# Sixteen state readouts in a decoder step: four fused multiply-sums on VectorE become one wide product there and four summing copies on ScalarE

## The chip, the cores and the metric

The kernel runs on one core of one Trainium2 chip. The metric is the device time of one execution in microseconds (us), as the median of several runs; smaller is better. The core has a matrix engine (TensorE, PE in the profile), a vector engine (VectorE, DVE), a scalar engine (ScalarE, ACT), GpSimd (POOL) and SyncE (SP), which issues most of the DMA transfers here. Each engine works through its own stream of instructions in order, and the engines meet at semaphores.

## The reference, cut to what matters

One step of a decoder trunk: a half-step SwiGLU FFN, a mixer (causal pooling beside a Mamba-2 SSD scan), a second half-step FFN, a final RMSNorm. It is computed for 512 prompt tokens and for 8 sample sequences of one new token each. Their 520 columns go through all products together. The sample rows have a stored SSD state of their own, 16 heads x 64 x 128 per sequence, and for one token the scan is one update and one readout:

```
h_new = exp(dt*A) * h0 + (dt * x) outer B          # per sequence b, head, 64 x 128
y     = sum over the 128 states n of  C[n] * h_new[.., n]
      = exp(dt*A) * (sum_n C[n] * h0[.., n]) + (dt * x) * (sum_n B[n] * C[n])
```

The kernel uses the second form of `y`. The sum over n of `C[n] * h0[.., n]` is the **readout** that is changed. B and C are shared by the heads of a group, of which there are two.

## The kernel before, in words

Features lie on the partitions, tokens along the free dimension, in two halves of 260 columns. Products with large weights are split: a weight tile is loaded raw by SP (`load_unit`, L111 to L114), `split` writes its rounded high part on ScalarE (L107) and the remainder on VectorE (L108), and three matmuls (`mm3`, L117 to L119) replace an fp32 product. Three high and three low buffers hold a unit each, so the cast of a unit can run once the unit three before it has been used.

The mixer's order is written out by hand as plans. The change works within this one:

```python
GATE_PLAN = (
    "A4 z0 B3 z1 m3 z2 B4 z3 s2 A5 z4 s2 B5 A6 z5 s2 s2 G0 z6 A7 z7 B6 s2 o0 H0 s2 o1 B7 s2 o2 s2 G1 "
    "o3 g0 g1 H1 g2 g3"
)
```

- `z` is a product of the gate's input projection, evacuated by two multiplications on VectorE (L916). `A` and `B` are the two halves of an SSD chunk: `ssd_a` makes decay matrices by exponentials on ScalarE (L861 to L871) and a large product on VectorE (L877), `ssd_b` multiplies with them on PE and combines on VectorE (L899 to L907).
- `s2` does two samples. `sample(b, g)` (L789) loads the row C of sequence b and group g, repeated over all partitions (`cb`, 128x128, L791), and the four 128x128 state blocks of that group (`h0`, L793), and reads out each block into one column of `ysm`: one VectorE instruction per block that multiplies, writes the product to a tile nobody reads (`junk`) and gives the row sums (L796). In the profile each is two rows, SCALAR_TENSOR_TENSOR and DVE_READ_ACCUMULATOR. There are 16 samples (8 sequences by 2 groups), so 64 readouts. `h0` has four buffers, `cb` shares three with other small tiles.
- `G` (`gate`, L932) begins with `sample_y`, which combines the readouts of one group (L802 to L804), adds them to the sample columns of X (L940) and multiplies by the gate (L942). `G0` needs the first eight samples, `G1` the last eight.
- `H` (`gate_out`, L944) takes squares on ScalarE (L948), sums them over partitions with a matmul of ones (`psr_y`, L161), makes the reciprocal root (L162 on ScalarE, L163 on VectorE) and writes the normalized, split operand `catg` (L955 to L957).
- `o`, `g`, `h` are output products over the pooling part, the first and the second half of the SSD part: units of four groups of 12 matmuls, each group added into the residual on VectorE (L926). `g` needs the `catg` of H0. `h`, which opens the last plan (`LAST_PLAN`), needs that of H1.

A planner lays out every engine's stream when the kernel is built: it plays the program against its own costs for instructions and takes, on each engine, the earliest instruction of the program that is ready by its clock. So an engine's stream isn't the program's order, and it is fixed before the run. `tc.keep_in_program_order(ins)` pins an instruction behind the one that the program issued last on the same engine. Later instructions may still be planned between pinned ones. Each of the 64 readouts is pinned so, behind the readout or other VectorE instruction before it.

Of the kernel before, what the change touches and what calls it, by code (L numbers as in the profile page):

```python
# [11 lines left out]
AF = mybir.ActivationFunctionType  # L12
ALU = mybir.AluOpType
# [3 lines left out]
P = 128  # L17
# [543 lines left out]
def mixer(tc, ins, outs, e):  # L561
    nc = tc.nc
# [191 lines left out]
    ysm = mp.tile([P, NX, NS], F32, tag="ysm", name="ysm")  # L754
    sbc = mp.tile([P, 2, NS], F32, tag="sbc", name="sbc")
    junk = act.tile([P, NT], F32, tag="acc", name="junk")[:, :P]
    scr_bc = dr.tile([NS, 512], F32, name="scr_bc")

    def rows_bc(b, a, g):
        return scr_bc.rearrange("b (a g n) -> b a g n", a=2, g=2)[b, a, g].unsqueeze(0).to_broadcast([P, P])  # L760
# [28 lines left out]
    def sample(b, g):  # L789
        cb = tmp.tile([P, HB], F32, tag="ta", name=f"cb{b}{g}")[:, :P]  # L790
        nc.sync.dma_start(out=cb, in_=rows_bc(b, 1, g))  # L791
        h0 = mp.tile([P, 4, P], F32, tag="h0", bufs=4, name=f"h0_{b}{g}")
        nc.sync.dma_start(out=h0, in_=ins["state_ssm"][:, b, 4 * g : 4 * g + 4])  # L793
        for q in range(4):
            tc.keep_in_program_order(
                nc.vector.scalar_tensor_tensor(out=junk, in0=h0[:, q], scalar=1.0, in1=cb, op0=ALU.mult, op1=ALU.mult,  # L796
                                               accum_out=ysm[:, 4 * g + q, b : b + 1]))

    def sample_y(g):
        gs = slice(4 * g, 4 * g + 4)  # L800
# [161 lines left out]
    def samples(n):  # L962
        for _ in range(n):
            if smp:
                sample(*smp.pop(0))
# [134 lines left out]
```

## Time and profile before

| | |
|---|---|
| median of 3 runs | 1006.09 us (1003.35, 1006.09, 1006.34) |
| the profiled execution | 1003.51 us, of which the span is 1000.5 us |
| mean granted TensorE clock | 0.994 |
| busy: PE, VectorE, ScalarE, GpSimd | 971.7, 806.9, 528.7, 87.8 us |
| instructions on VectorE and ScalarE | 1408 and 881 |

The span runs from the first to the last instruction of the profiled execution; 3 us of its time lie outside. Busy time is an average over stages with different limits, so the stretch in which the changed lines run has to be looked at for itself. Matmuls overlap one another, and a busy PE row says only that some matmul was under way. In timelines the columns are the start in us, the duration in us, the engine and line, the operation, the tiles and shapes, the number of merged instructions, and in brackets the idle time before the row and what ended it. In tables by stretch, each row has the length of the stretch and then the busy us of each engine in it, with the number of instructions.

### The profile page before, as it was taken

What the parts mean: (1) busy time and instruction counts of PE and PEld (TensorE: products, weight loads), DVE (VectorE), ACT (ScalarE), POOL (GpSimd) and SP (SyncE); (2) the same over time, 40 slices, a digit from 0 to 9 for tenths busy, and PEclk for the clock granted to TensorE, in tenths of its full rate; (3) what the DMA queues carried; (4) which work ended last, traced back from release to release, by engine and by line L of the source; (5) the groups of instructions that cost most, each with busy time, mean ns of one, the idle gap of its engine ahead of it and who ended that gap; (6) DMA issues with size and microseconds to landing.
All of it is one profiled execution on the core that took longest, in us unless ns stands there. A gap on an engine that the chain in (4) does not pass through costs nothing.

```text
span 1000.5 us, 19362 instructions
## 1 busy us (share of the span) xinstructions
PE 971.7 (97%) x7850; PEld 951.4 (95%) x7850; DVE 806.9 (81%) x1408; ACT 528.7 (53%) x881; POOL 87.8 (9%) x157
## 2 busy tenths in 40 slices
PE   7999999999999999999999999999999999999994
PEld 6899999999999999999899998899999999999993
DVE  7999657996569688788979987999957999668865
ACT  7566414664145455684845235666743666436552
POOL 0000000000000000167312000100012000120000
PEclk9999999999999999999999999999999999999997
DMA  6333232323223223263334421423346333452213
GB/s 194 112 126 114 98 101 73 124 88 124 85 85 106 85 104 117 87 216 105 107 133 122 146 90 54 124 94 118 127 137 187 120 127 118 124 195 96 95 33 85
DMA packets 44072, 114.44 MB, mean 114 GB/s; under 512 B 6408, under 2 KB 15560, under 8 KB 43984
## 3 DMA queue, kind: packets, MB, share of 16 engines
q1 hardware_dynamic: 40912, 103.78, 30.7%
q0 software_dynamic: 3072, 9.44, 3.5%
q8 instruction: 61, 1.00, 0.4%
q14 instruction: 27, 0.22, 0.1%
HBM read 105.86 MB, written 7.34 MB: 113 GB/s over the span
## 4 chain that ended last, share of the span: by engine, by line
PE 88%; DVE 6%; ACT 2%; POOL 2%; issue 1%; DMA 0%; SPq 0%; DVEq 0%; ACTq 0%
PE A L119 8%; PE A L117 8%; PE A L118 8%; PE dn L117 7%; PE dn L119 7%; PE dn L118 7%; PE BE L117 6%; PE BE L119 6%; PE BE L118 6%; PE P L232 4%; PE wo L117 2%; PE wo L118 2%; PE wo L119 2%; PE inz L117 2%; PE inz L119 2%; PE inz L118 2%
## 5 line engine op out<-in xcount | busy, mean ns | idle before, releaser
L117 PE MATMUL dn<-g,whi_1d 128*128 128x260 f32 x352 | 99.3, 283 | 0.2 <-DVE td L367 0.2
L118 PE MATMUL dn<-g,whi_1d 128*128 128x260 f32 x352 | 99.5, 283 | 0.0
L119 PE MATMUL dn<-g,wlo_1d 128*128 128x260 f32 x352 | 99.4, 283 | 0.0
L367 DVE SCALAR_TENSOR_TENSOR td<-dn,r_f 128x520 f32<-128x520 f32 x40 | 27.9, 699 | 73.2 <-PE dn L119 73.2
L119 PE MATMUL dn<-g,wlo_2d 128*128 128x260 f32 x256 | 72.4, 283 | 0.0
L118 PE MATMUL dn<-g,whi_2d 128*128 128x260 f32 x256 | 72.3, 282 | 0.0
L117 PE MATMUL dn<-g,whi_2d 128*128 128x260 f32 x256 | 72.3, 282 | 0.0
L117 PEld LDWEIGHTS dn<-g,whi_1d 128*128 128x128 f32 x352 | 66.1, 188 | 0.4 <-DVE td L367 0.4
L118 PEld LDWEIGHTS dn<-g,whi_1d 128*128 128x128 f32 x352 | 66.3, 188 | 0.0
L119 PEld LDWEIGHTS dn<-g,wlo_1d 128*128 128x128 f32 x352 | 66.2, 188 | 0.0
L297 ACT COPY ac<-A 128x260 f32<-128x260 f32 x123 | 45.6, 374 | 29.3 <-PE A L119 28.0
L107 ACT CAST whi_1d<-raw_1d 128x1024 fp32r<-128x1024 f32 (+1 forms) x24 | 23.4, 980 | 67.0 <-PE dn L118 54.2
L260 DVE TENSOR_TENSOR s<-raw 128x1024 f32<-128x1024 f32 x41 | 50.0, 1220 | 3.9 <-DMA raw<-in_w2gu 3.9
L232 PE MATMUL P<-xg_f,raw 128*128 128x260 f32 x192 | 45.1, 392 | 6.2 <-DMA raw<-in_w1gu 5.4
L232 PEld LDWEIGHTS P<-xg_f,raw 128*128 128x128 f32 x192 | 36.9, 195 | 12.1 <-ACT xg_f L179 5.4
L117 PEld LDWEIGHTS dn<-g,whi_2d 128*128 128x128 f32 x256 | 48.3, 189 | 0.0
L118 PEld LDWEIGHTS dn<-g,whi_2d 128*128 128x128 f32 x256 | 48.2, 188 | 0.0
L119 PEld LDWEIGHTS dn<-g,wlo_2d 128*128 128x128 f32 x256 | 48.2, 188 | 0.0
L118 PE MATMUL wo<-catg,whi_wo 128*128 128x260 f32 x128 | 36.4, 285 | 1.3 <-DVE catg L957 1.3
L117 PE MATMUL wo<-catg,whi_wo 128*128 128x260 f32 x128 | 37.3, 292 | 0.3 <-DVE h L926 0.3
L117 PE MATMUL inz<-xh_mx,whi_inz 128*128 128x260 f32 x128 | 36.8, 287 | 0.1
L117 PE MATMUL inx<-xh_mx,whi_inx 128*128 128x260 f32 x128 | 36.4, 284 | 0.0
(1340 smaller groups left out, 3924.1 us busy)
## 6 DMA issues: line engine op xcount, KB each, us to landing
raw<-in_w2gu SPq DMA_DIRECT2D x44, 512.0 KB, 4.5
raw<-in_w1gu SPq DMA_DIRECT2D x42, 512.0 KB, 4.4
raw_1d<-in_w1d SPq DMA_DIRECT2D x16, 512.0 KB, 4.4
raw_2d<-in_w2d SPq DMA_DIRECT2D x16, 512.0 KB, 4.6
raw_wo<-in_w_out SPq DMA_DIRECT2D x12, 512.0 KB, 5.0
ab<-scr_acs SPq DMA_DIRECT2D x8, 512.0 KB, 4.8
h<-in_state_ssm SPq DMA_DIRECT2D x16, 256.0 KB, 4.2
raw_inz<-in_w_in SPq DMA_DIRECT2D x8, 512.0 KB, 3.9
```

What stands on the lines that cost most here:

```text
L107: nc.scalar.copy(h, src)
L117: nc.tensor.matmul(ps, whi, xhi, start=start, stop=False, **kw)
L118: nc.tensor.matmul(ps, whi, xlo, start=False, stop=False, **kw)
L119: nc.tensor.matmul(ps, wlo, xhi, start=False, stop=stop, **kw)
L232: nc.tensor.matmul(self.banks[f, u][b][:, :HB], ws(self.raw[f][:, u], j + 4 * q), xg[:, slot[q]], start=j == q == 0, stop=j == 3 and q == ...
L260: nc.vector.tensor_tensor(out=s1, in0=diag, in1=up0, op=ALU.add)
L297: nc.scalar.copy(keep, out[:, :HB])
L367: nc.vector.scalar_tensor_tensor(out=t, in0=banks[d][:, :, :HB], scalar=-0.5, in1=self.nx[3].rearrange("p (b t) -> p b t", b=2), op0=ALU.mult,
```

## The change

Per sample, one VectorE multiplication over all four blocks (128x512, C repeated along the blocks) is written over the state tile `h0`. Four ScalarE copies then read one block each, write it to `junk`, and give its row sum into `ysm`. All five are pinned to program order on their engines. Loads, buffers, plans and everything else stay.

```diff
         h0 = mp.tile([P, 4, P], F32, tag="h0", bufs=4, name=f"h0_{b}{g}")
         nc.sync.dma_start(out=h0, in_=ins["state_ssm"][:, b, 4 * g : 4 * g + 4])
+        tc.keep_in_program_order(
+            nc.vector.tensor_tensor(out=h0, in0=h0, in1=cb.unsqueeze(1).to_broadcast([P, 4, P]), op=ALU.mult))
         for q in range(4):
             tc.keep_in_program_order(
-                nc.vector.scalar_tensor_tensor(out=junk, in0=h0[:, q], scalar=1.0, in1=cb, op0=ALU.mult, op1=ALU.mult,
-                                               accum_out=ysm[:, 4 * g + q, b : b + 1]))
+                nc.scalar.activation(out=junk, in_=h0[:, q], func=AF.Copy,
+                                     accum_out=ysm[:, 4 * g + q, b : b + 1]))
```

## The prediction

> **What bounds the kernel now.** I read the page's busy times first, then the waits of PE, then a table by stretch around the readouts.
>
> ```profile
> span 1000.5 us, 19362 instructions
> PE 971.7 (97%) x7850; PEld 951.4 (95%) x7850; DVE 806.9 (81%) x1408; ACT 528.7 (53%) x881; POOL 87.8 (9%) x157
> ```
>
> PE is busy 971.7 of 1000.5 us, so all the idle time that any change off PE could win in the whole span is 28.8 us. The next view is the table of who waited for whom, for PE, from 400 to 620 us, which is the mixer and the output products. Its columns are the total wait in us, the number of waits and the longest.
>
> ```profile
> PE psr_y L161 <- ACT X L948: 1.6, 1, 1.6
> PE wo L118 <- DVE catg L957: 1.3, 2, 0.6
> PE px L849 <- DVE xdt L873: 0.7, 1, 0.7
> PE pb L841 <- DVE U L604: 0.6, 1, 0.6
> PE wo L117 <- DVE h L926: 0.3, 1, 0.3
> ```
>
> Three of these five belong to what follows the second combination of readouts, G1 and H1: the sum of squares `psr_y` (1.6), the normalized operand `catg` (1.3) and one addition to the residual (0.3). Together they are 3.2 us, and that is the most this change can win at PE. Where the readouts stand is shown by the busy times by stretch (length, then busy us and instruction count of each engine), cut at the first readout, the first combination at 539.1, the pause of the readouts, the normalization of H0, the second combination at 582.1, and PE's last wait. The second fence is the same table for the readout line alone.
>
> ```profile
> 511.40:539.10 27.70, 27.70 (x236) 26.77 (x235) 27.18 (x97) 12.88 (x20) 6.33 (x5) 1.00 0.47 141
> 539.10:547.80 8.70, 8.70 (x76) 7.77 (x75) 8.63 (x22) 6.38 (x7) 3.50 (x1) 1.00 0.31 108
> 547.80:564.60 16.80, 16.80 (x130) 15.40 (x130) 16.28 (x35) 6.83 (x9) 1.53 (x1) 1.00 0.25 83
> 564.60:582.10 17.50, 17.50 (x147) 17.50 (x147) 16.42 (x74) 3.15 (x3) 0.00 (x0) 1.00 0.51 171
> 582.10:605.70 23.60, 20.45 (x149) 18.95 (x147) 19.32 (x35) 9.06 (x13) 0.00 (x0) 1.00 0.21 75
> ```
>
> ```profile
> 511.40:539.10 27.70, 10.88 (x64) 1.00 0.47 141
> 547.80:564.60 16.80, 1.93 (x14) 1.00 0.25 83
> 564.60:582.10 17.50, 7.39 (x50) 1.00 0.51 171
> sum 94.30, DVE 20.20; mean DVE 4.04
> ```
>
> Two things are to be seen. VectorE (third engine number) is full from 511 to 582: 27.18 of 27.70, 8.63 of 8.70, 16.28 of 16.80, 16.42 of 17.50. The readouts are 20.20 us of that. ScalarE (fourth number) has room. But PE (first number) is full too, in each of the four stretches, and at a granted clock of 1.00. VectorE's load there is hidden behind PE. It comes to light only after 582.1, where PE is busy 20.45 of 23.60 us: 3.15 us idle, which is the 3.2 of the waits above. The timelines of VectorE, ScalarE and PE show how the last readout leads to the first of these waits.
>
> ```profile
> 581.30 0.29 DVE L796 SCALAR_TENSOR_TENSOR junk<-h,cb 128x128 f32<-128x128 f32 x1
> 581.63 0.29 DVE L796 SCALAR_TENSOR_TENSOR junk<-h,cb 128x128 f32<-128x128 f32 x1
> 582.07 0.43 DVE L926 TENSOR_TENSOR h<-wo,h 128x260 f32<-128x260 f32 x1
> 582.41 0.18 DVE L803 TENSOR_TENSOR ysm<-ysm,sdec 128x32 f32<-128x32 f32 x1
> 583.42 0.70 DVE L942 TENSOR_TENSOR zs<-X,zs 128x520 f32<-128x520 f32 x1
> 584.34 2.61 ACT L948 ACTIVATE X<-zs 128x520 f32<-128x520 f32 x4
> 585.03 1.15 PE L161 MATMUL psr_y<-X,ones 128*128 128x260 f32 x4 [1.56 <-ACT X L948]
> ```
>
> The last readout starts at 581.63, the combination follows at 582.41, the gate product at 583.42, the squares at 584.34, and PE, which has waited 1.56 us, goes on at 585.03. So the readouts bound the kernel in one place, G1, and for about 3 us.
>
> **The change part by part.** *VectorE, removed and added.* The readouts and the two nearest rows for the product:
>
> ```profile
> L796 DVE SCALAR_TENSOR_TENSOR junk<-h,cb x64: 227/286/1135, 511.5 to 581.6; 128x128 f32<-128x128 f32 x64
> L796 DVE DVE_READ_ACCUMULATOR junk<-h,cb x64: 75/82/91, 511.7 to 581.8; 128x1 f32 x64
> L903 DVE TENSOR_TENSOR E<-yd,E 128x512 f32<-128x512 f32 x3 | 2.0, 677 | 0.0
> L877 DVE TENSOR_TENSOR ab<-ab,scm x8: 1211/1215/1833, 436.3 to 536.7; 128x1024 f32<-128x1024 f32 x8
> ```
>
> A product of 128x512 took 677 ns at L903 (one operand in PSUM). L877 has both operands in SBUF and one repeated, as here, and its 1215 ns for twice the width give 608. I take 0.68. So 64 readouts, 20.20 us, give way to 16 products, 16 x 0.68 = 10.9 us: VectorE is relieved of 9.3 us. Before the first combination that is 10.88 - 8 x 0.68 = 5.4 us, and between 547.8 and 582.1 it is 1.93 + 7.39 - 8 x 0.68 = 3.9 us. At once this is worth nothing, since PE is full in these stretches. What is worth something is that the chain into G1 starts up to 3.9 us sooner, as VectorE ran almost without a gap to get there.
>
> *ScalarE, added.* 64 copies with a row sum. The trace has no such instruction on ScalarE; these are the nearest rows (minimum, median, maximum ns):
>
> ```profile
> L866 ACT ACTIVATE ab<-ab,tok x32: 385/387/402, 429.9 to 527.5; 128x128 f32<-128x128 f32 x32
> L844 ACT COPY bt<-pb x8: 243/257/266, 431.0 to 533.7; 128x128 f32<-128x128 f32 x8
> L856 ACT ACTIVATE we<-we x8: 192/209/211, 429.8 to 516.9; 128x8 f32<-128x8 f32 x8
> ```
>
> The lower end is a plain 128x128 copy with the sum free, 0.26 us (L844). The upper end is the ACTIVATE of 128x128 followed by a read of the sum as dear as a whole small ACTIVATE, 0.387 + 0.209 = 0.60. I take the ACTIVATE with a read like VectorE's 82 ns, 0.387 + 0.082 = 0.47, because L866 is the same engine, opcode, shape and memory. That is 64 x 0.47 = 30 us on ScalarE in all. The Trainium skill, page "ScalarE: Activation LUTs", section "What ACT_TABLE_LOAD costs", gives 186 ns + 0.833 ns per element for an ACTIVATE without pointer operands and about 93 ns more for each of them; its 280 + 107 = 387 ns with one agrees with L866. By that page the copy alone would be an estimated 293 ns, with the read 0.375, and the gain below would be 2.4 us in place of 2.0.
>
> In the first stretch ScalarE has 12.88 us of work in 27.70, and 32 readouts add 15.0: 27.9. So it fits by a hair. There is some slack behind it, in the rows of H0:
>
> ```profile
> 543.51 2.20 ACT L948 ACTIVATE X<-zs 128x520 f32<-128x520 f32 x4
> 547.98 2.35 PE L161 MATMUL psr_y<-X,ones 128*128 128x260 f32 x10
> ```
>
> The squares of H0 end at 545.71 and PE takes them up at 547.98, so G0 may be 2.3 us late before PE feels it. I cost this part at nothing; the cover is gone from (27.7 + 2.3 - 12.88) / 32 = 0.54 us per readout, waits for products included. In the second half ScalarE has 6.83 + 3.15 us of work in 34.3, and 15.0 more fit easily.
>
> *The waits that are added.* Each group of four copies waits for its product on VectorE, and queued behind it on ScalarE are the casts of weights (L107), the exponentials and the squares; VectorE's remainders (L108) wait for the casts, and PE for both. The casts can bear it:
>
> ```profile
> ACT whi_wo L107 <- PE wo L118: 13.6, 4, 4.7
> ```
>
> They themselves wait up to 4.7 us for PE to free a buffer, the third one back, so two units of PE work lie between a cast and its use. The combination (L803) now waits for ScalarE, with additions to the residual (L926) and remainders queued behind it on VectorE. At G1 this costs the four last copies after the last product, 4 x 0.47 = 1.9 us.
>
> *SP.* Its stream of loads has weights behind the sample loads, and it waits for the readouts:
>
> ```profile
> SPq L791 <- DVE junk L796: 22.4, 8, 8.5
> SPq L113 <- DVE junk L796: 17.2, 3, 10.7
> ```
>
> A state buffer is now freed by ScalarE's fourth copy, a `cb` already by the product. The same weights are still due in the same order; I cost it at nothing, as the buffers come free with the samples and these run earlier, not later. If a sample were freed later, loads of output weights (L113) would be late with it.
>
> *The sum.* G1 comes 3.9 - 1.9 = 2.0 us sooner. PE's 3.2 us after it are one chain's lateness, so 2.0 of it go: psr_y's 1.6 first, and 0.4 of `catg`. After that PE is the bound to the end. On the profiled execution's own time: 1003.51 - 2.0 = 1001.5 us. That execution lies 2.6 below the median of 1006.09, among runs from 1003.35 to 1006.34, so the forecast for a median is 1006.09 - 2.0 = **1004.1 us**. With the read at 0.26 the gain would be 3.9 - 1.0 = 2.9, at 0.60 it would be 1.5.
>
> **The rivals.** *The whole idle time goes.* Before, each of the 64 pinned readouts let another VectorE instruction in between, as the addition at 582.07 between the last two rows above; now the chain has 16 turns. Then the last products could follow the last addition of o2 directly and G1 would come more than 3.2 us sooner: 1006.09 - 3.2 = 1002.9. For it speaks that ScalarE is busy only 3.15 us of the last 17.5; against it that the planner, not the hardware, decides the order, and that the state loads have four buffers.
>
> *Nothing is gained.* The streams are laid out by the planner's clock. PE waited at 585.03 because it was told to take `psr_y` there, and a new plan can be early by the same amount. Then the time stays at 1006.1.
>
> *Slower: ScalarE is late at the first combination.* It decides from 0.54 us per readout. At 0.60 and with every product exposed once (ScalarE standing still for 8 x 0.68 = 5.4 us while VectorE, which is full, gets to it) the stretch needs 12.88 + 19.2 + 5.4 = 37.5 us; less 27.7 and the slack of 2.3 that is 7.5 us at PE, less the 1.5 gained at G1: 1012.1. With half the exposure it is 3.3 us, 1009.4. For it speaks that my 0.47 is close to the limit; against it that PE has the products of o0 to o2 to do, which don't need H0's operand, if the plan puts them first. The same ScalarE page, section "Rules for kernel authors", would have additions and multiplications on VectorE, not ScalarE, which is this rival's side; no row before shows a sum on ScalarE.
>
> **How the numbers follow.** What a measurement of this kernel can tell from no change is about 0.3%, 3.0 us. Chances: the forecast 0.38 (its own range 1003 to 1005.5), nothing gained 0.14, the whole idle time 0.20, slower 0.28. The forecast and "nothing" are within 0.3%, together 0.52; faster 0.20; slower 0.28. The range reaches from 1001.0 (the fastest run shown, 1003.35, less the forecast's 2.0, rounded down) to 1010.0, which takes in the slower rival to half its exposure.
>
> **What would show it.** VectorE's busy time falls by about 9 us and ScalarE's rises by about 30; products read 0.61 to 0.68 us, copies with their read 0.26 to 0.60. PE's waits for the squares and for `catg` after G1 shrink from 2.9 us to about 1. If they stay, the planner's order decides. If PE or VectorE waits around the first combination for ScalarE's copies, the slower rival is right. The forecast is wrong if a wait for weights appears at PE, or if the sum on ScalarE costs more than 0.6 us.

## The result, and the profile after

The changed kernel takes 999.51 us (median of 6 runs, 998.63 to 1000.05). The kernel before takes 1003.69 us (median of 6, 1002.22 to 1006.34). The ratio is 0.9953, with a 95% interval from 0.9942 to 0.9965: faster, by about 4.7 us (the two medians differ by 4.2). The forecast was a gain of 2.0 us, and the time lies below its range. Its number, 1004.1, also started from a three-run median of 1006.09, which six runs moved down by 2.4 us.

The profiled execution took 1000.05 us. These are the first lines of its page.

```profile
span 996.8 us, 19404 instructions
PE 970.9 (97%) x7850; PEld 951.5 (95%) x7850; DVE 799.0 (80%) x1296; ACT 552.5 (55%) x1009; POOL 87.3 (9%) x157
```

PE has the same 7850 matmuls and nearly the same busy time as before (970.9 and 971.7 us), in a span that is 3.7 us shorter. VectorE lost 7.9 us of busy time and ScalarE gained 23.8. The waits of PE between 400 and 620 us (total, number, longest) are now these:

```profile
PE pb L843 <- DVE U L604: 1.0, 1, 1.0
PE px L851 <- DVE xdt L875: 0.7, 1, 0.7
PE pm L118 <- DVE catp L737: 0.3, 1, 0.3
```

The three waits behind G1 and H1, for `psr_y`, for `catg` and for `h`, are gone altogether. What is left lies ahead of the samples. The table by stretch, with the cuts of the prediction, shows the same from the side of the busy times:

```profile
511.40:539.10 27.70, 27.70 (x237) 26.77 (x236) 22.05 (x39) 24.37 (x82) 6.62 (x5) 1.00 0.41 126
539.10:547.80 8.70, 8.70 (x75) 7.77 (x75) 8.66 (x22) 7.22 (x10) 3.29 (x1) 1.00 0.49 178
547.80:564.60 16.80, 16.80 (x131) 15.40 (x129) 14.34 (x22) 9.61 (x25) 1.32 (x1) 1.00 0.31 102
564.60:582.10 17.50, 17.50 (x148) 17.50 (x147) 16.21 (x37) 13.00 (x53) 0.00 (x0) 1.00 0.41 132
582.10:605.70 23.60, 23.60 (x182) 23.05 (x182) 20.21 (x33) 10.28 (x15) 0.00 (x0) 1.00 0.28 91
```

PE (first) is full in all five stretches; before, the last one had 20.45 of 23.60 us. VectorE (third) has 5.7 us of air in the first stretch and 2.5 in the third; ScalarE (fourth) has taken the work and is not full anywhere. The new instructions cost this (minimum, median, maximum ns, then the first and last start):

```profile
L798 ACT ACTIVATE junk<-h x64: 290/311/313, 516.2 to 579.0; 128x128 f32<-128x128 f32 x64
L798 ACT ACTIVATION_READ_ACCUMULATOR junk<-h x64: 185/187/195, 516.4 to 579.2; 128x1 f32 x64
L795 DVE TENSOR_TENSOR h<-h,cb x16: 676/681/694, 512.3 to 575.4; 128x512 f32<-128x512 f32 x16
```

The end of the last readouts, on ScalarE and then on VectorE (start, duration, engine and line, operation, tiles, and in brackets the idle time and what ended it):

```profile
575.04 1.04 ACT L107 CAST whi_wo<-raw_wo 128x1024 fp32r<-128x1024 f32 x1
575.98 0.31 ACT L798 ACTIVATE junk<-h 128x128 f32<-128x128 f32 x1
...
579.02 0.31 ACT L798 ACTIVATE junk<-h 128x128 f32<-128x128 f32 x1
579.24 0.19 ACT L798 ACTIVATION_READ_ACCUMULATOR junk<-h 128x1 f32 x1
579.33 1.03 ACT L107 CAST whi_wo<-raw_wo 128x1024 fp32r<-128x1024 f32 x1
581.41 2.47 ACT L950 ACTIVATE X<-zs 128x520 f32<-128x520 f32 x4 [1.04 <-DVE zs L944]
```

```profile
570.91 1.28 DVE L795 TENSOR_TENSOR h<-h,cb 128x512 f32<-128x512 f32 x2
...
575.39 0.69 DVE L795 TENSOR_TENSOR h<-h,cb 128x512 f32<-128x512 f32 x1 [0.24 <-DMA cb<-scr_bc]
576.00 0.76 DVE L928 TENSOR_TENSOR h<-wo,h 128x260 f32<-128x260 f32 x2
576.67 1.22 DVE L108 TENSOR_TENSOR wlo_wo<-raw_wo,whi_wo 128x1024 fp32r<-128x1024 f32 x1
577.80 0.76 DVE L928 TENSOR_TENSOR h<-wo,h 128x260 f32<-128x260 f32 x2
579.46 0.19 DVE L805 TENSOR_TENSOR ysm<-ysm,sdec 128x32 f32<-128x32 f32 x1 [0.90 <-ACT junk L798]
```

The last product is done at 576.08. ScalarE is behind by then and works off eight readouts from 575.98 to 579.43, 3.45 us or 0.43 each. VectorE uses that time for additions and a remainder until 578.56, and stands idle for 0.90 us only. The combination starts at 579.46, and the squares end at 581.41 + 2.47 = 583.88. PE takes them up right after:

```profile
583.97 0.28 PE L119 MATMUL wo<-catg,wlo_wo 128*128 128x260 f32 x1
584.08 3.67 PE L161 MATMUL psr_y<-X,ones 128*128 128x260 f32 x16
587.40 0.47 PE L117 MATMUL wo<-catg,whi_wo 128*128 128x260 f32 x1
```

All 16 `psr_y` matmuls run as one block with no wait. The first of them needs only the first of the four squares, which is done at 582.05, so PE has about 2.0 us in hand. Before the change it was the same: PE went on at 585.03 while the squares ran on until 586.95.

### The profile page after: what moved, and what is told of

It reads as the page before. It is cut to its first block, busy times and chain, and to the rows that moved or that the text cites. A ratio compares the mean times of both kernels' runs of the same rounds, so it can differ in the third digit from the quotient of the medians.

```text
span 996.8 us, 19404 instructions
## 1 busy us (share of the span) xinstructions
PE 970.9 (97%) x7850; PEld 951.5 (95%) x7850; DVE 799.0 (80%) x1296; ACT 552.5 (55%) x1009; POOL 87.3 (9%) x157
## 4 chain that ended last, share of the span: by engine, by line
PE 88%; DVE 5%; DMA 2%; POOL 1%; ACT 1%; issue 1%; SPq 0%; DVEq 0%; ACTq 0%
PE A L119 8%; PE A L117 8%; PE A L118 8%; PE dn L119 7%; PE dn L117 7%; PE dn L118 7%; PE BE L117 6%; PE BE L119 6%; PE BE L118 6%; PE P L232 4%; PE wo L117 2%; PE wo L119 2%; PE wo L118 2%; PE inz L117 2%; PE inz L119 2%; PE inz L118 2%
## 5 line engine op out<-in xcount | busy, mean ns | idle before, releaser
L117 PE MATMUL dn<-g,whi_1d 128*128 128x260 f32 x352 | 99.3, 283 | 0.2 <-DVE td L367 0.2
L117 PE MATMUL wo<-catg,whi_wo 128*128 128x260 f32 x128 | 37.2, 290 | 0.0
L119 PE MATMUL wo<-catg,wlo_wo 128*128 128x260 f32 x128 | 36.3, 283 | 0.0
```

The source lines that it names most:

```text
L117: nc.tensor.matmul(ps, whi, xhi, start=start, stop=False, **kw)
L119: nc.tensor.matmul(ps, wlo, xhi, start=False, stop=stop, **kw)
```

## The experiments

To compare runs whose PE is early or late by up to a microsecond at the start of the gate, I measure how late G1 is against PE's own progress: the second start of the combination (`ysm<-ysm,sdec`, last start) less the first start of a gate matmul (`inz`, first start). The first fence holds the two rows before, the second those after.

```profile
L803 DVE TENSOR_TENSOR ysm<-ysm,sdec x2: 183/188/192, 539.0 to 582.4; 128x32 f32<-128x32 f32 x2
L117 PE MATMUL inz<-xh_mx,whi_inz x128: 277/282/394, 482.0 to 538.9; 128*128 128x260 f32 x128
```

```profile
L805 DVE TENSOR_TENSOR ysm<-ysm,sdec x2: 182/187/192, 539.8 to 579.5; 128x32 f32<-128x32 f32 x2
L117 PE MATMUL inz<-xh_mx,whi_inz x128: 278/282/394, 482.8 to 539.6; 128*128 128x260 f32 x128
```

Before it is 582.4 - 482.0 = 100.4 us, after it is 579.5 - 482.8 = 96.7: G1 comes 3.7 us sooner.

My theory ("load") after the result: VectorE's work ahead of the second combination sets when G1 runs; the change takes enough of it away that PE meets no wait, and any further relief is worth nothing. The rival ("turns"): it is not the work but the number of pinned instructions, 16 for 64, which lets others in between. A third ("plan"): another order of the same work would have done as much. All experiments in one table; the waits are those up to 620 us, and the ratio is to the kernel before on the same chip.

| kernel | G1 against PE, us | PE's waits after G1, us | median, us | ratio (95%) |
|---|---|---|---|---|
| before | 582.4 - 482.0 = 100.4 | 3.2 | 1003.69 | 1 |
| after | 579.5 - 482.8 = 96.7 | none | 999.51 | 0.9953 (0.9942 to 0.9965) |
| again | 580.2 - 483.5 = 96.7 | none | 999.14 | 0.9953 (0.9941 to 0.9966) |
| turns_only | 584.3 - 482.5 = 101.8 | 4.3 | 1007.79 | 1.0038 (1.0025 to 1.0052) |
| second_only | 579.4 - 483.4 = 96.0 | none | 998.44 | 0.9949 (0.9936 to 0.9961) |
| first_only | 582.2 - 482.9 = 99.3 | 2.0 | 1002.14 | 0.9982 (0.9972 to 0.9992) |
| plan_early | 584.0 - 483.5 = 100.5 | 3.1 | 1003.91 | 1.0007 (0.9998 to 1.0016) |
| late_g1 | 578.9 - 482.2 = 96.7 | none | 998.66 | 0.9948 (0.9934 to 0.9962) |
| no_readouts_pinned | 569.9 - 482.1 = 87.8 | none | 998.03 | 0.9952 (0.9938 to 0.9966) |
| loaded_second | 584.8 - 482.4 = 102.4 | 3.7 | 1005.60 | 1.0025 (1.0014 to 1.0037) |
| half_double_act | 585.3 - 482.1 = 103.2 | 4.8 | 1005.93 | 1.0033 (1.0022 to 1.0045) |
| double_act | 599.4 - 482.3 = 117.1 | 15.5 at both | 1019.91 | 1.0167 (1.0152 to 1.0183) |

Where G1 comes at 96.7 or sooner, PE has no wait and the kernel is 0.5% faster, however much sooner it is. From 99.3 on PE waits. Among the slow ones the order isn't strict: turns_only, at 101.8, loses more than loaded_second at 102.4, and PE's wait was the longer one in it (4.3 against 3.3). What PE waits for is the first square, and other work of VectorE can come between the combination and that. Counted like G1, PE is ready for the first square at 101.3 in the runs with no wait, and it is done at 99.3 in the changed kernel, 103.0 in the kernel before, 104.7 in loaded_second and 105.8 in turns_only. no_readouts, which isn't in the table, has a different order of work and is told below.

**again.** The changed kernel once more, beside the next three.

> The changed kernel once more, beside the others of this call. Both theories: 3.5 to 4.7 us faster than before (0.9953 to 0.9965); its waits for squares and catg after G1 are absent in the profile.

The ratio is the same to the fourth digit. PE's first gate matmul is at 483.5 here and at 482.8 in the first profile of the same program, so 0.7 us of a difference between two spans can be how a run came to this place.

**turns_only.** The product stays, and the four sums are made on VectorE too, by one reduction per sample. Two pinned instructions for four, and no work leaves VectorE.

```diff
-        for q in range(4):
-            tc.keep_in_program_order(
-                nc.scalar.activation(out=junk, in_=h0[:, q], func=AF.Copy,
-                                     accum_out=ysm[:, 4 * g + q, b : b + 1]))
+        tc.keep_in_program_order(
+            nc.vector.tensor_reduce(out=ysm[:, 4*g:4*g+4, b], in_=h0, op=ALU.add, axis=mybir.AxisListType.X))
```

> Product and sums both on VectorE: one product of 128x512 and one reduction of 128x4x128 per sample, so 32 pinned instructions in place of 128, and about 16 x (0.68 + 0.65) = 21 us of VectorE, as much as before (20.2). Theory 'load' (the gain is VectorE's relief of 9 us): no gain, within 1 us of before, PE waits of about 3 us after G1 stay. Theory 'turns' (the gain is that fewer pinned instructions stand in VectorE's stream, each of which let another in between): 2 to 4 us faster, waits after G1 mostly gone.

```profile
L797 DVE TENSOR_REDUCE ysm<-h x16: 628/671/679, 514.3 to 582.5; 128x4 f32<-128x512 f32 x16
```

A reduction costs as much as a product, so a sample takes about 1.35 us on VectorE, about as much as its four fused readouts did. The pinned instructions are halved, and the kernel is slower, 1.0038. PE waits 4.3 us at G1. The turns theory falls. The load theory had expected no loss of more than 1 us; the loss is larger because the first square comes later still, and because PE's clock falls after the wait (last section).

**second_only and first_only.** The new readout for one group alone. The diff is that of second_only; first_only has `g == 1`.

```diff
+        if g == 0:
+            for q in range(4):
+                tc.keep_in_program_order(nc.vector.scalar_tensor_tensor(..., accum_out=ysm[:, 4 * g + q, b : b + 1]))
+            return
```

> The new readouts for group 1 alone (the last eight samples), the old ones for group 0. Theory 'G1' (only the start of the second combination is late for PE, the first is covered by PE's work): the whole gain or more, 3.5 to 5 us, as G1 is reached sooner and nothing is put on ScalarE before G0. Rival 'load anywhere' (VectorE's backlog from 511 us on is what makes G1 late, so relief in the first half counts as well): about half, 1.5 to 2.5 us.

> The new readouts for group 0 alone. Theory 'G1': no gain, within 1 us of before, PE's waits after G1 stay at about 3 us. Rival 'load anywhere': 1.5 to 2.5 us faster, the waits after G1 about halved.

The two lines are the last stretch of the table by stretch, in second_only and in first_only.

```profile
582.10:605.70 23.60, 23.60 (x185) 23.13 (x184) 19.82 (x31) 9.41 (x15) 0.00 (x0) 1.00 0.27 90
```

```profile
582.10:605.70 23.60, 21.58 (x159) 20.20 (x159) 19.50 (x37) 8.78 (x13) 0.00 (x0) 1.00 0.24 87
```

Group 1 alone fills PE and gives the whole gain, 0.9949. Group 0 alone brings G1 1.1 us sooner and gives 0.9982; PE is busy 21.58 of 23.60 us, against 20.45 before. The first combination isn't sooner for it: 539.9 - 482.9 = 57.0, as before the change. Most of the 5 us by which VectorE is relieved in the first stretch is lost there, since it then waits for PE and, with its remainders, for casts on ScalarE (1.7 and 1.3 us). The first square of H1 is no sooner either, 103.0, and the wait for it stays at 1.6 us; the wait for `catg` shrinks from 1.3 to 0.4. I had expected no gain from group 0; the 0.18% is what the rival "load anywhere" had expected of this run, but not of second_only, where it wanted half the gain.

**plan_early.** The kernel before, with the last samples one plan step earlier and no other change.

```diff
-    "... B6 s2 o0 H0 s2 o1 B7 s2 o2 s2 G1 "
+    "... B6 s2 o0 s2 H0 s2 o1 B7 s2 o2 G1 "
```

> The kernel before with its old readouts, and only the plan changed: of the last eight samples, two move from behind o2 to behind B6/o0, so that G1's readouts are pinned behind earlier work. Theory 'G1' (the gain is that the second combination starts sooner, whatever the engine): 2 to 4.5 us faster than before with not one instruction changed, the combination some us sooner, the waits for squares and catg smaller. Rival 'load' in its strict form (VectorE is full, so the same work in another order ends as late): within 1 us.

PE's waits after G1 are 1.6 us for `psr_y`, 1.2 for `catg` and 0.3 for `h`; before they were 1.6, 1.3 and 0.3. But this is no other order: the planner made the same streams of the edited plan. The traces of the two kernels show the same work on every engine, in the same order, and the same loads on SP. So the run repeats the kernel before, and whether another order would have done as much is not tested.

**late_g1.** The changed kernel, with G1 asked for one output unit later.

```diff
-    "... B7 s2 o2 s2 G1 o3 g0 g1 H1 g2 g3"
+    "... B7 s2 o2 o3 s2 G1 g0 g1 H1 g2 g3"
```

> The changed kernel with its last two samples behind o3 in place of o2 in the plan: VectorE and ScalarE have the same work, but the last products are pinned behind o3's additions. Theory 'G1': the combination comes 2 to 5 us later than in the changed kernel, the waits for squares come back, and 2 to 4 us of the gain are lost (0.9975 to 0.999 of before). Theory 'load': the gain stays (0.995).

The combination comes at 96.7 as before the edit, and the time stays at that of the changed kernel. VectorE's stream did change a little: the last product starts at 576.21 - 482.2 = 94.0, where it was 575.39 - 482.8 = 92.6. That this delays nothing shows what sets G1 in the changed kernel. In its profile ScalarE makes 24 readouts and two casts from 567.2 to 579.4 with no pause above 0.2 us, and the combination waits for the last of them. So after the change G1 waits for ScalarE's row of readouts, which begins when VectorE has made the product of 566.5, and the products inside the row have some time in hand.

**no_readouts and no_readouts_pinned.** What is left when the readouts cost nothing: two tiny copies per sample free the buffers, not pinned in the first kernel and pinned in the second. Both leave out the sums, so `y` of the sample rows is not the reference's. The edit is shown against the changed kernel.

```diff
-        tc.keep_in_program_order(
-            nc.vector.tensor_tensor(out=h0, in0=h0, in1=cb.unsqueeze(1).to_broadcast([P, 4, P]), op=ALU.mult))
-        for q in range(4):
...
+        nc.vector.tensor_copy(ysm[:, 4 * g : 4 * g + 4, b], h0[:, :, 0])
+        nc.vector.tensor_copy(junk[:, 0:1], cb[:, 0:1])
```

> Leaves out all 64 readouts (ysm gets one column of the state, so y of the sample rows is not the reference's); the loads stay. The ceiling of anything done to the readouts. Theory 'G1': 3.5 to 5 us faster than before, no more than the changed kernel within 1 us, since PE has no wait left after G1 there. Rival 'VectorE bounds more than that': more than 6 us faster.

The first missed: it was slower than before, 1008.94 us, ratio 1.0050 (1.0036 to 1.0063). Its copies were laid out far ahead of their place, with the combinations at 446.2 and 459.4, and VectorE's stream stood there for the loads. These are rows of the waits of VectorE, then of PE, in that run between 400 and 640 us.

```profile
DVE junk L795 <- DMA cb<-scr_bc: 4.0, 5, 1.5
...
DVE ysm L794 <- DMA h<-in_state_ssm: 2.0, 2, 1.3
```

```profile
PE yo L884 <- DVE hst L897: 2.5, 1, 2.5
PE yd L890 <- DVE U L602: 1.8, 1, 1.8
```

So PE waits in the scan in place of G1, its clock falls to half for 10.2 us behind the wait of 2.5 (last section), and the run is no measure of the ceiling. The second is one:

> The readouts left out again (y of the sample rows is not the reference's), now with two tiny copies per sample pinned to the readouts' place in the program, where the run before let them move ahead to 446 us and VectorE's stream waited there for loads. Theory 'load' with the ceiling at G1: no wait of PE upstream of the samples, none after G1, 3.5 to 5 us faster than before (0.995 to 0.9965), no better than the changed kernel by more than 1 us. Rival 'VectorE bounds more': below 0.994.

```profile
582.10:605.70 23.60, 23.60 (x180) 22.95 (x179) 17.71 (x28) 9.19 (x13) 0.00 (x0) 1.00 0.22 81
```

G1 comes 8.9 us sooner than in the changed kernel, VectorE does 2.5 us less in this stretch, and the ratio is 0.9952 against 0.9953. With PE full there is nothing more to be won from the readouts.

**loaded_second.** The changed kernel with one more product of 128x512 (by ones) per sample of group 1, which puts about what the change took from VectorE back on it.

```diff
+        if g == 1:
+            tc.keep_in_program_order(
+                nc.vector.tensor_tensor(out=h0, in0=h0, in1=ones.unsqueeze(1).to_broadcast([P, 4, P]), op=ALU.mult))
```

> The changed kernel with one more VectorE product per sample of group 1: the state tile times a tile of ones, pinned behind the real product (the result stays the same). It gives VectorE back 8 x 0.6 = 4.8 us ahead of G1 and changes nothing on ScalarE. Theory 'load' (VectorE's amount of work ahead of G1 sets the start of the second combination): the combination comes 4 to 5 us later than in the changed kernel, PE's waits for squares and catg come back, 3 to 5 us are lost: 0.999 to 1.001 of before. Rival 'planner' (it is the place in the streams or the pins that were changed, not the load): the gain stays within 1 us, 0.9945 to 0.9965.

```profile
PE psr_y L161 <- ACT X L953: 3.3, 1, 3.3
```

This is the longest of PE's waits from 560 to 620 us (two more are of 0.2): they come back with the load. G1 is 2.0 us later than before the change, and the time is 1.0025, more than I had expected of it. Two reasons are at hand, and neither is shown: ScalarE's tail comes on top of VectorE's load, and PE's clock may fall in some executions (last section). The profile is of the fastest of the eleven, 1003.07 us at a mean granted clock of 0.994; the slowest, 1009.51, had 0.989.

**half_double_act and double_act.** The changed kernel with a plain ScalarE copy ahead of every second summing copy, and of each, to find where the slower rival of the prediction begins.

```diff
+            if q % 2 == 0:
+                tc.keep_in_program_order(nc.scalar.activation(out=junk, in_=h0[:, q], func=AF.Copy))
```

> The changed kernel with one plain copy more ahead of every second summing copy on ScalarE, half of what double_act added. double_act's PE waits were 15.5 us; the readout there costs about 0.435 + 0.21 = 0.65 us, here 0.54, the point from which the prediction had ScalarE late at the first combination. Theory 'threshold at 0.54': PE waits 0 to 2 us at the first sum of squares and little after G1, 0.996 to 1.000 of before. Rival 'any load on ScalarE costs in proportion': half of double_act's loss against the changed kernel, about 10 us, 1.005 of before.

> The changed kernel with a second, plain copy of 128x128 on ScalarE ahead of each summing copy: about 64 x 0.21 to 0.31 = 13 to 20 us more on ScalarE, 0.65 to 0.75 us per readout, over the 0.54 from which the prediction had ScalarE late at the first combination. By that rival: 32 x 0.70 + 12.9 = 35.3 us of work in a stretch of 27.7 + 2.3, so PE waits about 5 us at the first sum of squares, and the tail at G1 grows: 2 to 6 us slower than before. Rival 'cover is larger' (PE takes other work first, and H0's operand isn't due for 7 us): faster than before still, by 0 to 3 us, G1's tail alone costing.

PE's waits from 500 to 620 us, in the half dose:

```profile
PE psr_y L161 <- ACT X L952: 4.4, 1, 4.4
PE wo L118 <- DVE catg L961: 0.4, 1, 0.4
```

and in the full dose:

```profile
PE psr_y L161 <- ACT X L951: 15.5, 2, 9.5
```

With the half dose the first combination is at 542.3, 3.3 us later than before, and PE doesn't feel it; the single wait for squares is at G1. So my threshold of 0.54 us per readout missed, and the loss, 1.0033, is nearer to the rival's 1.005. With the full dose it is at 551.6, PE waits at both, and the loss of 17 us is far above the 2 to 6 that I had expected. ScalarE late is a real way to lose here, but it shows first at G1, and the cover at the first combination is more than 3 us.

## Why the prediction was wrong

The place and the direction were right, the size was not. By its own steps:

- **G1 as the one bound: right.** All that PE gained lies behind G1, and the readouts of group 1 alone give it (second_only).
- **VectorE's relief: the sign right, the size too high.** The product was 681 ns against 0.68. But 1.93 + 7.39 us is the busy time of the readouts' rows, and the read at the end of a readout overlaps what follows. In the kernel before, a readout between two additions took 0.23 us from start to next start:

```profile
580.39 0.28 DVE L796 SCALAR_TENSOR_TENSOR junk<-h,cb 128x128 f32<-128x128 f32 x1
580.60 0.08 DVE L796 DVE_READ_ACCUMULATOR junk<-h,cb 128x1 f32 x1
580.62 0.43 DVE L926 TENSOR_TENSOR h<-wo,h 128x260 f32<-128x260 f32 x1
```

Counted so, with idle time apart, the second group's readouts took 8.0 us before and its products 4.8 after (0.60 each): 3.2 us in place of 3.9.
- **ScalarE's readout: right within the bounds.** 0.43 us for 0.47, 25.7 us of busy time on that line for 30. The two parts were wrong in opposite senses, a copy of 0.31 for 0.387 and a read of 0.19 for 0.082. The estimate from the Trainium skill's page "ScalarE: Activation LUTs", section "What ACT_TABLE_LOAD costs", was 293 ns for the copy; the rows are 290 to 313 with a median of 311, so the least agrees and the median lies 18 ns above it.
- **The tail was the step that failed first**: "At G1 this costs the four last copies after the last product, 4 x 0.47 = 1.9 us." ScalarE did run 3.4 us past the last product, eight readouts and not four. But the step counted ScalarE's tail as if VectorE stood still in it. VectorE had four additions and a remainder to do, and idled 0.90 us.
- **The sum took the rest of VectorE's stream as fixed.** Between the two combinations VectorE took 582.4 - 539.0 = 43.4 us before and 579.5 - 539.8 = 39.7 after, the 3.7 by which G1 is sooner, and not 3.9 - 1.9 = 2.0. The readouts give 3.2 of that. In the new streams only 18 additions and 5 remainders stand ahead of G1, where it was 23 and 6, which gives 2.8. Against it the idle time rose from 1.7 to 3.8, by 2.1: the tail's 0.9 and, around H0, waits for ScalarE's root and a cast (1.74 and 0.72). What is left, 0.2, is small changes. In turns_only and loaded_second 24 additions and 6 remainders stand ahead of G1, so they go behind it only where the readouts leave VectorE room. How much the work alone would have won in the old order isn't shown; no run held the order fixed.
- **The cap of 3.2 us was too small.** "Together they are 3.2 us, and that is the most this change can win at PE" reads the wait column as the loss. It is not all of it. PE before the change, at one of the `catg` waits:

```profile
600.21 0.28 PE L117 MATMUL wo<-catg,whi_wo 128*128 128x260 f32 x1
601.12 0.39 PE L118 MATMUL wo<-catg,whi_wo 128*128 128x260 f32 x1 [0.63 <-DVE catg L957]
601.34 0.28 PE L119 MATMUL wo<-catg,wlo_wo 128*128 128x260 f32 x1
601.46 0.28 PE L117 MATMUL wo<-catg,whi_wo 128*128 128x260 f32 x1
```

Matmuls follow each other at 0.12 us (601.34 to 601.46). From 600.21 to 601.12 are 0.91 us, so 0.79 are lost, and the row says 0.63, because a matmul's duration of 0.28 overlaps its successor's. The restart costs 0.10 more (601.12 to 601.34 is 0.22). Counted so from start to start over all the places behind G1, PE lost about 4.4 us. The same stretch of PE's work, 336 output matmuls and the 16 of `psr_y`, from the first `wo` start behind the last chunk of the scan (560.13, then 560.91) to the first start of the product that follows them (608.60, then 604.96), took 48.47 us before and 44.05 after, 4.4 less. Of that, the spans show 3.7, as PE came to the gate 0.8 us later in this run (482.8 for 482.0), which is within what the same program does from run to run (again: 483.5; plan_early, which is the kernel before: 483.5).
- **So a rival held**, "the whole idle time goes", with 4.4 us for its 3.2, and G1 did come more than 3.2 us sooner, partly by overtaking additions as that rival said. But the number of turns alone doesn't do it: turns_only was slower. The wait for the first square was 1.6 us, G1's 3.7 cover it with about 2.0 to spare, and the waits and restarts behind it go too.
- **The slower rival's place was wrong.** The first combination has more cover than the 2.3 us that I read from H0's squares, since I took the end of the last square and PE needs only the first. That one ended at 544.13, 3.9 us before PE went on at 547.98, and 3.3 us of delay at the combination cost PE nothing. ScalarE's readouts decide at G1, where with a half dose more of copies the kernel took 1.0033 of the time before.
- **SP and the casts: right.** PE has no wait for a weight in the rows after, and the casts on ScalarE run between the readouts (575.04 and 579.33 above).
- **The base.** The median of three runs, 1006.09, was 2.4 us above that of six. Without this the forecast would have been 1001.7. By its own rule (the fastest run less 2.0, rounded down) the range would have begun at 1000.0, and the result, 999.51, would still lie below it.

What stays open: why loaded_second spreads from 1003.07 to 1009.51 (only its fastest run was profiled), and whether some other hand-written order of the kernel before would have filled PE too; the one that was tried came out as the same program.

## What to carry to other kernels

Work that is moved from a full engine to one with room is worth no more than what the bound engine loses by waiting for it: here VectorE lost 7.9 us of work, G1 came 3.7 us sooner, and 4.4 us of loss on PE ended there; even with no readouts at all nothing further was won. Read the cover of such a place from the first result that the bound engine needs, not from the end of the row. When a moved tail is priced, ask what the old engine does meanwhile, and charge only the idle time that is left. Count what a pipelined engine loses from start to start against its own pitch, since the wait column leaves out the overlap and the restart. And when an edit of a plan changes nothing in the time, look first whether it changed the streams.

## What the runs showed of the hardware that was not expected

**PE's clock can fall after one wait, and the length of the wait doesn't decide it.** In turns_only PE waited 4.33 us at G1. These are three stretches of 3.41 us, the first of which ends where the clock falls (length, busy us and number of matmuls of PE, then the granted clock, the share of DMA and GB/s):

```profile
582.77:586.18 3.41, 1.17 (x10) 1.00 0.89 309
586.18:589.59 3.41, 1.32 (x3) 0.50 0.03 6
589.59:593.00 3.41, 3.41 (x16) 0.50 0.00 0
```

The clock is 0.50 from 586.18 to 593.00 and 1.00 after it. PE's timeline shows the price:

```profile
588.27 2.10 PE L161 MATMUL psr_y<-X,ones 128*128 128x260 f32 x4 [4.33 <-ACT X L948]
590.38 0.42 PE L118 MATMUL wo<-catg,whi_wo 128*128 128x260 f32 x1
590.60 0.42 PE L119 MATMUL wo<-catg,wlo_wo 128*128 128x260 f32 x1
```

A matmul takes 0.42 us for 0.28, and one follows the other after 0.22 for 0.12. In loaded_second, after a wait of 3.3 us, the clock holds, and in no_readouts it falls after a wait of 2.5. The first fence is loaded_second, the second no_readouts.

```profile
582.38:585.79 3.41, 1.56 (x13) 1.00 0.79 269
585.79:589.20 3.41, 1.98 (x13) 1.00 0.13 48
```

```profile
478.92:482.34 3.42, 0.93 (x9) 1.00 0.78 287
```

The stretches are cut where the clock itself can switch. Between 400 and 620 us the clock stays at half for 6.83 us in turns_only, 3.41 in half_double_act, 10.24 in no_readouts, and 6.83 and 10.24 in double_act: once, twice or three times 3.41. All rises and falls there lie on steps of 3.413 us counted from the first rise of the clock in the same trace, and loaded_second is cut on its own steps. In the step that ends with a fall PE was busy 34% (turns_only), 20% (half_double_act), 27% (no_readouts) and not at all (double_act, twice). Steps with 46% and 58% (loaded_second), 51% (half_double_act) and 54% (before) ended with no fall. So in these traces a fall goes with a step in which PE was busy little, the limit lies somewhere between 34% and 46%, and it matters how a wait lies on the steps. By that the same wait can cost more in one execution than in another, which would fit loaded_second's spread but isn't shown for it. The Trainium skill, page "TensorE: Matmul & The Clock Gate", section "Part 1: The HAM clock gate (the "warmup" mystery)", gives half rate after at least one idle window of about 3.4 us, in windows that run freely. The traces agree with the windows, but PE wasn't idle for the whole of one in turns_only (34% busy), and there the measurement decides.

**The read of a sum is dearer on ScalarE**: 187 ns against 82 on VectorE. In a row, a summing copy on ScalarE comes every 0.43 us, and a fused readout on VectorE came every 0.33 (581.30 to 581.63).
